# Modulation weights of the feed-forward stage: places of their own, GpSimd's queue, and arithmetic moved to VectorE

## The chip, the cores and the metric

One core of a Trainium2 chip runs the whole program. Its engines are TensorE (PE, with its weight loads as PEld), VectorE (DVE), ScalarE (ACT), GpSimd (POOL) and SyncE (SP). Transfers are issued from the queues of SP, ACT and POOL. The metric is the device time of one execution in microseconds (us); the time of a kernel is the median of its runs.

## What is computed

One step of a two-layer backbone over 384 tokens (128 of context, 256 latent) of width 1024. Each layer is a mixing part and a channel part; the change lies in the channel part and in the modulation that all parts use:

```python
def _modulation(cond, w, b):
    m = jax.nn.silu(cond) @ w + b
    return m.reshape(cond.shape[0], N_MOD, D_MODEL)      # six rows of 1024 for a layer

def _block(x, mod, lw, mix):
    h = _rms(x, g[0]) * (1 + mod[:, None, 1]) + mod[:, None, 0]
    y, aux = mix(h)
    x = x + mod[:, None, 2] * _rms(y @ lw['w_out'], g[1])
    h = _rms(x, g[2]) * (1 + mod[:, None, 4]) + mod[:, None, 3]
    f = jnp.square(jax.nn.relu(h @ lw['ffn_w1'])) @ lw['ffn_w2']
    return x + mod[:, None, 5] * _rms(f, g[3])
```

The weights are float32: w1 and w2 are 1024 x 4096 and 4096 x 1024, and a layer's modulation matrix is 1024 x 6144. Every input is read from HBM once in a run.

## The kernel before, in words

**Dense products.** A float32 weight is cut into units of 128 x 1024 (512 KB). `fetch` (L367) loads a unit into a place named ws or dws (SP, L372), copies it to a rounded high part wh or dwh on ACT, and subtracts to get the low part wl or dwl (`split`, L332 and L320). A product is then three matmuls: high x high, high x low, low x high. The low parts go in turn to the engines in `self.low`: V and P (DVE, POOL) in the dense stages by `P['ld']`, V, V, P in the mixing stage by `P['lm']`. Inside a dense stage the places alternate between a static pool (three ws, two wh, two wl) and one opened by `open_dense` (two dws, four dwh, four dwl).

**The feed-forward stage** (`ffn`, L1670) runs 33 turns. Turn j makes hidden block j with `fm` (24 matmuls of 384 columns into a bank named pd), then Relu on ACT, the square on DVE and a split into f (low part on DVE for even j, on POOL for odd j), and adds hidden block j-1 to the output rows with `rows_product` (18 matmuls of 512 columns into pr and pm). The last four blocks and the norms stand in `dense_end`, which goes through the three tiles of 128 tokens one after another: `postnorm` (residual added half on POOL, half on DVE), then `prenorm` for the next part, whose low parts hl are made on POOL for the first half of the columns.

**Modulation.** One half of a chunk (512 columns of the modulation matrix) is `mod_sums` (L539): four loads of 512 KB into ws and dws places (SP, L545) and eight products with the 32-column cstat; then `mod_turn` copies the sums, transposes them and adds the bias. The first four halves run ahead of layer 0 in `start`, six more halves beside mixing 0. Feed-forward 0 carries twelve halves (chunk 5 of its own layer and five chunks of the next), feed-forward 1 carries two.

**Order.** `merge` interleaves generators by a planner's clock: each yield adds a cost. The modulation generator starts at 28 and its costs are multiplied by 6.5; `presplit` starts at 6 and costs 7.2 a unit. `presplit` loads the 29 input-projection units of layer 1 (SP, L387), splits them and stores the low parts to HBM (SP, L390, the tile low); mixing 1 then loads these. A turn of the feed-forward stage costs 7.8. Each engine and each queue then works through its instructions in a fixed order, and an instruction that waits holds what stands behind it.

In this profile the start lasts to about 33 us, feed-forward 0 runs from 442 to 779 us, and feed-forward 1 from 1156 to 1437 us.

Of the kernel before, what the change touches and what calls it, by code (L numbers as in the profile page):

```python
# [10 lines left out]
F32 = mybir.dt.float32  # L11
# [3 lines left out]
ALU = mybir.AluOpType  # L15
# [153 lines left out]
MIX = (5120, 12544, 15584)  # L169


P = {'wq': [8, 1, 4], 'hp': (0, 400), 'np': 3, 'we': 1, 'dp': [], 'ka': 0, 'kk': [], 'pw': '', 'lm': 'VVP', 'ld': 'VP', 'mf': 6.5, 'pq': [0], 'na': 2, 'nb': 2, 'pe': 'VAVA', 'xw': 4, 'fo': 28, 'wt': 4, 'xs': 2, 'mo': 60, 'mr': 7.5, 'ps': 7.2, 'po': 6, 'rw': (1.4, 1.4), 'ao': (80, 100), 'ar': (1.7, 1.4), 'so': (120, 120), 'sr': (1.4, 1.7), 'ho': (0, 0), 'hr': (0.8, 0.9), 'hl': (4, 4), 'lv': (2.0, 2.0), 'ul': (1, 1), 'rw0': 1.4, 'ao0': 80, 'ar0': 1.7, 'so0': 100, 'sr0': 1.4, 'ho0': 0, 'hr0': 0.9, 'hl0': 6, 'lv0': 4.0, 'ul0': 2, 'rw1': 1.4, 'ao1': 100, 'ar1': 1.7, 'so1': 120, 'sr1': 1.7, 'ho1': 0, 'hr1': 0.9, 'hl1': 4, 'lv1': 2.0, 'ul1': 3}


def par(name, l):
    return P.get(f"{name}{l}", P[name][l])

# [104 lines left out]
class Builder:  # L282
    def __init__(self, nc, tc, pools, io, dbg=None, places=None):
        self.places, self.arenas = places, []
        self.nc, self.tc, self.io, self.dbg = nc, tc, io, dbg
        self.pools = pools
        self.nunit = 0
        self.lows = {}
        self.ready = []
        self.xs, self.xw, self.ntail = P['xw'], 4, 4  # L290
        self.wsets = {n: [(pools[n], n)] for n in ("ws", "wh", "wl")}
        self.turn = {n: 0 for n in self.wsets}
        self.low = (nc.vector, nc.vector, nc.gpsimd)
        self.phase, self.side = None, ExitStack()
# [11 lines left out]
    def pw(self, which):  # L306

        return self.pm() if self.win_left or str(which) not in P["pw"] else self.pd()

# [72 lines left out]
    def presplit(self, l):  # L382

        for n in (7, 8, 0, 2, 4, 1, 3, 5, 6, *range(9, 29)):
            st = self.pools["ws"].tile([128, 1024], F32, name="ws", tag="ws")
            h, lo = (self.pools[k].tile([128, 1024], F32R, name=k, tag=k) for k in ("wh", "wl"))
            self.nc.sync.dma_start(st, self.io["win"][l, n])  # L387
            self.split(h, lo, st)
            d = self.pools["spl"].tile([128, 1024], F32, name=f"low{n}", tag=f"low{n}")
            self.nc.sync.dma_start(d, lo.bitcast(F32))  # L390
            self.lows[l, n] = d
            yield P["ps"]

# [10 lines left out]
    def close(self):  # L404
        if self.phase is not None:
            self.phase.close()
        self.phase = None
        self.static_slots()

    def static_slots(self):  # L410
# [31 lines left out]
    def open_dense(self):  # L442
        self.close()
        self.phase = ExitStack()
        self.low = [{"V": self.nc.vector, "P": self.nc.gpsimd}[x] for x in P["ld"]]
        n = MIX[1] - 4 * 4 * T
        a = self.pool("da", 1)
        self.fy = self.pool("db", 1)
        self.tmp = self.arena([a.tile([128, n], F32, name="tmp")], [n]).get
        p = self.pools  # L450
        for n, k, order in (("ws", self.xs, (0, 1)), ("wh", self.xw, (0, 1, 1)), ("wl", self.xw, (0, 1, 1))):
            q = self.pool("d" + n, k)
            self.wsets[n] = [((p[n], n), (q, "d" + n))[o] for o in order]
# [85 lines left out]
    def mod_sums(self, l, ch, hf):  # L539

        ps = self.pd()
        c0 = ch * 1024 + hf * 512
        for u in range(4):
            w = self.slot("ws", F32)
            self.nc.sync.dma_start(w, self.io["modw"][l, u * 256:u * 256 + 256, c0:c0 + 512].rearrange("(k p) n -> p k n", p=128))  # L545
            for k in range(2):
                n = u * 2 + k
                q = n % 4 * 32
                self.mm(ps[q:q + 32], self.cstat[:, n], w[:, k * 512:k * 512 + 512], n < 4, n >= 4)
        return ps  # L550
# [75 lines left out]
    def norm_out(self, t, q, ps, G, M, h):  # L626
        st = 0 if t == 0 else 1
        hb = self.tmp(512)
        h32 = hb.ap(4, 128)
        for j in range(4):  # L630
            k = q * 4 + j
            c = slice(j * 128, j * 128 + 128)
            if P["pe"][j] == "A":
                self.act(h32[:, j], ps[:, c], AF.Identity, scale=G[:, st, k:k + 1], bias=M[:, st, k:k + 1])
            else:
                self.ts(h32[:, j], ps[:, c], G[:, st, k:k + 1], M[:, st, k:k + 1], ALU.mult, ALU.add)
        sl = (slice(None), slice(q * 4, q * 4 + 4), slice(t * 128, t * 128 + 128))
        self.split(h[0][sl], h[1][sl], h32, self.nc.gpsimd if q in P["pq"] else None)
        hb.free()

    def postnorm(self, t, xt, acc, gate):
        sb = self.tmp(8)
        s = sb.ap(8)
        ub = self.tmp(1024)
        u = ub.ap(1024)
        st = 0 if t == 0 else 1
        for hf in range(2):
            self.act(u[:, hf * 512:hf * 512 + 512], acc[hf], AF.Square, accum_out=s[:, hf:hf + 1])
        self.tt(s[:, 2:3], s[:, 0:1], s[:, 1:2], ALU.add)
        self.rstd(s[:, 3:4], s[:, 2:3], 1.0 / D, 0)  # L650
        for hf in (1, 0):
            sl = slice(hf * 512, hf * 512 + 512)
            self.stt(u[:, sl], acc[hf], s[:, 3:4], gate[:, st, sl])
            self.tt(xt[:, sl], xt[:, sl], u[:, sl], ALU.add, self.nc.gpsimd if hf else None)
        ub.free()
        sb.free()

# [1009 lines left out]
    def wout(self, l):  # L1667
        yield from self.dense_end([self.wout_unit(l, n) for n in (0, 1)], (l, 3), None, [self.io["w1"][l, n] for n in range(P["na"])])

    def ffn(self, l, layers):  # L1670
        nc, io, h = self.nc, self.io, self.h
        fs = [self.fy.tile([128, 4, T], F32R, name=f"f{i}") for i in range(4)]
        self.acc = self.sums("rrrmmm")
        last = l == layers - 1
        tail = []
        for j in range(33):
            if j < 32:
                if j == 0:
                    first = self.fm_first([io["w1"][l, i] for i in range(2)], h)
                o = first[j] if j < 2 else self.fm(io["w1"][l, j], h)  # L1680
                rb = self.tmp(T)
                r = rb.ap(T)
                self.act(r, o, AF.Relu)
                self.tt(r, r, r)
                fh, fl = (fs[j // 4 % 2 * 2 + i][:, j % 4] for i in range(2))
                self.split(fh, fl, r, nc.gpsimd if j % 2 else nc.vector)
                rb.free()
                yield 3.9
            if j:
                n = j - 1  # L1690
                u = (io["w2"][l, n * 128:n * 128 + 128], [fs[n // 4 % 2 * 2 + i][:, n % 4] for i in range(2)])
                if n < 32 - self.ntail:
                    self.rows_product(self.acc, *u[1], self.unit(u[0]), n == 0, False)
                    yield 3.9
                else:
                    tail.append(u)
        self.spread_gate(l, 5)
        save = io["y"] if last else self.pools["dram"].tile([T, D], F32, name="xsave", tag="xsave")
        yield from self.dense_end(tail, None if last else (l + 1, 0), save, [] if last else [self.win_src(l + 1, U_R + n) for n in (7, 8)[:P["nb"]]])
        self.home = save  # L1700

    def build(self, layers=L):
        nc, io = self.nc, self.io
        self.open_x()
        self.open_dense()
        self.home = io["x"]
        self.setup()
        p = self.pools["h"]
        self.h = (p.tile([128, 8, T], F32R, name="hh"), p.tile([128, 8, T], F32R, name="hl"))

        def mod(l, chunks):
            for ch in chunks:
                yield from self.mod_chunk(l, ch)

        def later(chunks):
            for ch in chunks:
                yield from self.mod_chunk(*ch)

        self.start()
        for l in range(layers):  # L1720
            self.mix(l, [(P["mo"], P["mr"], mod(l, (2, 4, 3)), 0)] if l == 0 else [])
            self.run(self.wout(l))
            chunks = [(l, 5)] if l == layers - 1 else [(l, 5)] + [(l + 1, n) for n in (1, 0, 2, 4, 3)]
            self.merge(self.ffn(l, layers), (P["fo"], P["mf"], later(chunks), 0), *([(P["po"], 1.0, self.presplit(l + 1), 0)] if l < layers - 1 else []))
        self.close()
        self.side.close()

# [38 lines left out]
```

## Time and profile before

| | us |
|---|---|
| median of three runs (1448.27 to 1451.86) | 1451.23 |
| the profiled execution's own time | 1446.73 |
| its span, first to last instruction | 1444.9 |
| PE busy | 1297.9 |
| DVE busy | 778.8 |
| ACT busy | 637.6 |
| POOL busy | 396.2 |

The profiled execution is 4.5 us quicker than the median; 1.8 us of its time lie outside the span. Busy time is a sum over the engine's instructions and includes matmuls whose ends are modelled, so a stage is read by what PE waited for and by its pace, not by its busy share alone. A wait is put down to the instruction that came last.

### The profile page before, as it was taken

How to read it: one execution, taken by the hardware profiler on the slowest of the kernel's cores; microseconds unless marked ns; L12 is line 12 of the kernel's file. 1: busy time of each engine (PE TensorE's matmuls, PEld its weight loads, DVE VectorE, ACT ScalarE, POOL GpSimd, SP SyncE). 2: the span in 40 equal slices, each digit the busy share in tenths (PEclk: the TensorE clock that was granted, in tenths of full speed). 3: DMA queues.
4: the chain of work that ended last, by engine and by line, in shares of the span. 5: the costliest groups of instructions: out<-in, count | busy, mean ns of one | idle time of the engine just before them, and what ended most of it. 6: DMA issues, size and time to landing. Idle time of an engine off the chain costs nothing.

```text
span 1444.9 us, 21103 instructions
## 1 busy us (share of the span) xinstructions
PE 1297.9 (90%) x8294; PEld 1090.5 (75%) x8294; DVE 778.8 (54%) x1245; ACT 637.6 (44%) x1255; POOL 396.2 (27%) x288
## 2 busy tenths in 40 slices
PE   6997997899868999999997999879999599999997
PEld 2886686577657777678786988769876498999996
DVE  2689869734443434343544358886454543544443
ACT  4666533244344333344445568333444633333332
POOL 1224536000041123322333003650000422333332
PEclk8998999979986999999998999879999889999999
DMA  9431343621461588888864555216315426544411
GB/s 340 151 105 59 118 126 113 203 91 36 163 205 39 197 297 307 276 313 284 309 236 154 168 186 188 77 29 190 102 39 181 136 67 213 171 129 126 125 59 44
DMA packets 94644, 229.55 MB, mean 159 GB/s; under 512 B 24720, under 2 KB 27088, under 8 KB 94544
## 3 DMA queue, kind: packets, MB, share of 16 engines
q1 hardware_dynamic: 82448, 210.80, 44.0%
q10 hardware_dynamic: 11968, 17.37, 3.7%
q8 instruction: 65, 1.06, 0.3%
q14 instruction: 35, 0.29, 0.1%
q0 software_dynamic: 128, 0.03, 0.0%
HBM read 206.90 MB, written 21.27 MB: 158 GB/s over the span
## 4 chain that ended last, share of the span: by engine, by line
PE 45%; DVE 7%; DMA 7%; ACT 5%; POOL 2%; issue 2%; SPq 0%; ACTq 0%; POOLq 0%; DVEq 0%
PE pd L335 22%; PE pm L335 11%; PE pr L335 11%; DMA ws<-w 3%; DVE mix L320 3%; DMA low<-wl 1%; ACT tmp L329 1%; ACT mix L329 1%; DMA ws<-win 1%; DMA wl<-low 1%; PE pm L338 1%; POOL mix L320 1%; ACT wh L332 1%; ACT dwh L332 1%; DVE wl L320 1%
## 5 line engine op out<-in xcount | busy, mean ns | idle before, releaser
L335 PE MATMUL pd<-hh,wh 128*128 128x384 f32 (+2 forms) x656 | 228.0, 348 | 17.0 <-ACT hh L332 7.2
L335 PE MATMUL pd<-hh,wl 128*128 128x384 f32 (+2 forms) x656 | 227.3, 347 | 13.5 <-DVE wl L320 9.3
L335 PE MATMUL pd<-hl,wh 128*128 128x384 f32 (+2 forms) x656 | 225.5, 344 | 1.3 <-POOL hl L320 1.3
L332 ACT CAST wh<-ws 128x1024 fp32r<-128x1024 f32 x121 | 126.5, 1047 | 174.6 <-DMA ws<-win 70.8
L320 DVE TENSOR_TENSOR tmp<-tmp 128x384 f32<-128x384 f32 (+1 forms) x76 | 101.3, 1333 | 142.5 <-ACT tmp L329 142.4
L320 DVE TENSOR_TENSOR wl<-ws,wh 128x1024 fp32r<-128x1024 f32 x67 | 87.9, 1312 | 132.5 <-ACT wh L332 110.8
L320 DVE TENSOR_TENSOR mix<-mix 128x384 f32<-128x384 f32 (+21 forms) x249 | 143.7, 592 | 28.0 <-ACT mix L329 9.7
L335 PEld LDWEIGHTS pd<-hh,wh 128*128 128x128 f32 x656 | 129.4, 198 | 27.4 <-issue 8.6
L335 PEld LDWEIGHTS pd<-hh,wl 128*128 128x128 f32 x656 | 129.2, 197 | 21.1 <-DVE wl L320 10.3
L329 ACT ACTIVATE mix<-mix 128x384 f32<-128x384 f32 (+4 forms) x188 | 107.4, 599 | 56.6 <-DVE mix L320 34.9
L335 PEld LDWEIGHTS pd<-hl,wh 128*128 128x128 f32 x656 | 129.4, 197 | 3.3 <-POOL hl L320 1.8
L335 PE MATMUL pd<-hh,dwl 128*128 128x384 f32 (+2 forms) x368 | 126.0, 342 | 4.1 <-POOL dwl L320 4.1
L335 PE MATMUL pd<-hh,dwh 128*128 128x384 f32 (+2 forms) x368 | 125.8, 343 | 3.6 <-ACT hh L332 2.7
L335 PE MATMUL pd<-hl,dwh 128*128 128x384 f32 (+2 forms) x368 | 125.4, 341 | 1.8 <-POOL hl L320 1.8
L320 POOL TENSOR_TENSOR wl<-ws,wh 128x1024 fp32r<-128x1024 f32 x25 | 61.6, 2464 | 191.0 <-ACT wh L332 152.7
L320 POOL TENSOR_TENSOR mix<-mix,mix 64x384 f32<-64x384 f32 (+1 forms) x45 | 69.0, 1539 | 88.9 <-ACT mix L329 66.5
L320 POOL TENSOR_TENSOR dwl<-dws,dwh 128x1024 fp32r<-128x1024 f32 x22 | 52.8, 2403 | 125.7 <-ACT dwh L332 125.7
L335 PE MATMUL pr<-dwh,f 128*128 128x512 f32 x252 | 80.4, 400 | 4.1 <-ACT f L332 2.8
L335 PE MATMUL pm<-mix 128*128 128x128 f32 (+5 forms) x700 | 76.0, 268 | 8.5 <-POOL mix L320 5.4
L320 POOL TENSOR_TENSOR dwl<-ws,dwh 128x1024 fp32r<-128x1024 f32 x22 | 53.4, 2427 | 101.2 <-ACT dwh L332 101.2
L332 ACT COPY mix<-pr 32x384 f32<-32x384 f32 (+7 forms) x136 | 42.4, 336 | 83.5 <-PE pr L335 64.8
L335 PE MATMUL pm<-dwh,f 128*128 128x512 f32 x252 | 78.6, 391 | 0.0
(219 smaller groups left out, 2613.7 us busy)
## 6 DMA issues: line engine op xcount, KB each, us to landing
ws<-win SPq DMA_DIRECT2D x87, 512.0 KB, 4.6
dws<-w SPq DMA_DIRECT2D x64, 512.0 KB, 4.5
ws<-w SPq DMA_DIRECT2D x64, 512.0 KB, 4.4
ws<-modw SPq DMA_DIRECT2D x60, 512.0 KB, 4.8
dws<-modw SPq DMA_DIRECT2D x36, 512.0 KB, 6.5
low<-wl SPq DMA_DIRECT2D x29, 512.0 KB, 3.7
wl<-low SPq DMA_DIRECT2D x29, 512.0 KB, 3.7
ws<-wout SPq DMA_DIRECT2D x14, 512.0 KB, 4.1
```

What stands on the lines that cost most here:

```text
L320: (eng or self.nc.vector).tensor_tensor(out, a, b, op=op)
L329: self.nc.scalar.activation(out, a, fn, **kw)
L332: self.nc.scalar.copy(out, a)
L335: self.nc.tensor.matmul(out, l, r, start=start, stop=stop)
L338: self.nc.tensor.transpose(out, a, self.ident[:k, :k])
```

## The change

In the dense stages a pool of four places, wm, holds modulation weights alone, and their loads are issued on GpSimd's queue instead of SP's. That also covers the four halves of `start`, because `build` opens the dense pools before it; the six halves beside mixing 0 still use ws places and SP. In `ffn` the halves are no longer a merged generator: from turn 3 on every odd turn takes one half, its sums ahead of `rows_product` and its turning behind it, so that feed-forward 0 does its twelve in turns 3 to 25 and feed-forward 1 its two in turns 3 and 5. The store of presplit's low parts moves from SP's to GpSimd's queue. The low parts of dense units (`P['ld']` goes from 'VP' to 'V'), of f and of hl, and the residual add, all go to VectorE. The keys mf, fo and pq leave the table P. GpSimd's arithmetic in the mixing stage stays.

```diff
@@ presplit
-            self.nc.sync.dma_start(d, lo.bitcast(F32))
+            self.nc.gpsimd.dma_start(d, lo.bitcast(F32))
@@ close
-        self.phase = None
+        self.phase = self.wmod = None
@@ open_dense
+        self.wmod = self.pool("wm", 4)
         p = self.pools
@@ mod_sums
-            w = self.slot("ws", F32)
-            self.nc.sync.dma_start(w, self.io["modw"][l, u * 256:u * 256 + 256, c0:c0 + 512].rearrange("(k p) n -> p k n", p=128))
+            if self.wmod is not None:
+                w = self.wmod.tile([128, 1024], F32, name="wm", tag="wm")
+                q = self.nc.gpsimd
+            else:
+                w, q = self.slot("ws", F32), self.nc.sync
+            q.dma_start(w, self.io["modw"][l, u * 256:u * 256 + 256, c0:c0 + 512].rearrange("(k p) n -> p k n", p=128))
@@ norm_out
-        self.split(h[0][sl], h[1][sl], h32, self.nc.gpsimd if q in P["pq"] else None)
+        self.split(h[0][sl], h[1][sl], h32)
@@ postnorm
-            self.tt(xt[:, sl], xt[:, sl], u[:, sl], ALU.add, self.nc.gpsimd if hf else None)
+            self.tt(xt[:, sl], xt[:, sl], u[:, sl], ALU.add)
@@ ffn
-                self.split(fh, fl, r, nc.gpsimd if j % 2 else nc.vector)
+                self.split(fh, fl, r)
                 rb.free()
+                mod = halves.pop(0) if halves and j > 2 and j % 2 else None
+                if mod:
+                    ps = self.mod_sums(*mod)
                 yield 3.9
...
                     self.rows_product(self.acc, *u[1], self.unit(u[0]), n == 0, False)
+                    if mod:
+                        self.mod_turn(*mod, ps)
                     yield 3.9
@@ build
-            chunks = [(l, 5)] if l == layers - 1 else [(l, 5)] + [(l + 1, n) for n in (1, 0, 2, 4, 3)]
-            self.merge(self.ffn(l, layers), (P["fo"], P["mf"], later(chunks), 0), *([(P["po"], 1.0, self.presplit(l + 1), 0)] if l < layers - 1 else []))
+            chunks = [(l, 5)] + [(l + 1, n) for n in (1, 0, 2, 4, 3)] * (l < layers - 1)
+            self.merge(self.ffn(l, layers, [(*c, hf) for c in chunks for hf in range(2)]),
+                       *([(P["po"], 1.0, self.presplit(l + 1), 0)] if l < layers - 1 else []))
```

## Rows read from the trace of the kernel before

**Rows 1.** The page: PE's busy tenths in 40 slices of 36.1 us

```profile
PE   6997997899868999999997999879999599999997
```

**Rows 2.** Stretches: length, busy PE, PEld, DVE, ACT, POOL, clock, DMA share, GB/s

```profile
12.00:24.00 12.00, 9.24 (x60) 3.99 (x58) 4.29 (x23) 6.86 (x17) 0.00 (x0) 1.00 1.05 401
...
460.00:770.00 310.00, 297.37 (x1511) 240.45 (x1511) 130.28 (x133) 122.06 (x162) 89.18 (x47) 0.99 0.79 271
490.00:740.00 250.00, 237.74 (x1213) 187.39 (x1206) 108.87 (x112) 103.27 (x135) 74.05 (x39) 1.00 0.86 299
...
1162.00:1424.00 262.00, 262.00 (x1366) 235.83 (x1365) 120.11 (x86) 90.08 (x128) 86.68 (x47) 1.00 0.38 123
```

**Rows 3.** PE's waits from 454 to 770 us: total, times, longest

```profile
PE pd L335 <- POOL dwl L320: 4.1, 3, 1.5
PE pr L335 <- ACT f L332: 2.8, 2, 1.8
```

**Rows 4.** Waits of SP's DMA queue, 454 to 790 us

```profile
SPq L390 <- DVE wl L320: 80.4, 23, 10.1
...
SPq L545 <- POOL dwl L320: 18.2, 5, 5.7
```

**Rows 5.** Modulation matmuls (tile cstat): both feed-forward stages; PE busy is first

```profile
454.00:790.00 336.00, 29.52 (x192) 5.62 (x192) 0.00 (x0) 0.00 (x0) 0.97 0.75 258
1160.00:1300.00 140.00, 3.85 (x32) 0.83 (x32) 0.00 (x0) 0.00 (x0) 0.99 0.46 149
```

**Rows 6.** The chain in feed-forward 1, two pieces sixteen turns apart

```profile
1256.76 4.17 PE pd L335 x24
...
1390.52 4.24 PE pd L335 x24
```

**Rows 7.** Groups from 454 to 790 us: busy, mean ns, idle before

```profile
L320 POOL TENSOR_TENSOR dwl<-ws,dwh 128x1024 fp32r<-128x1024 f32 x20 | 48.6, 2429 | 98.4 <-ACT dwh L332 98.4
...
L320 DVE TENSOR_TENSOR dwl<-dws,dwh 128x1024 fp32r<-128x1024 f32 x19 | 35.9, 1908 | 31.4 <-ACT dwh L332 31.4
...
L320 POOL TENSOR_TENSOR wl<-ws,wh 128x1024 fp32r<-128x1024 f32 x9 | 22.5, 2496 | 57.8 <-ACT wh L332 50.4 <-DMA ws<-win 7.5
...
L320 POOL TENSOR_TENSOR f<-tmp,f 128x384 fp32r<-128x384 f32 x16 | 17.2, 1073 | 66.9 <-ACT f L332 66.9
```

**Rows 8.** Timeline: one low part on DVE while POOL is idle

```profile
487.67 1.23 DVE L320 TENSOR_TENSOR wl<-ws,wh 128x1024 fp32r<-128x1024 f32 x1 [3.95 <-ACT wh L332]
```

**Rows 9.** PE's waits, 400 to 460 us: total, times, longest

```profile
PE pd L338 <- DVE tmp L326: 14.6, 1, 14.6
...
PE pd L335 <- POOL hl L320: 1.8, 2, 0.9
```

**Rows 10.** Timeline inside the wait of 14.6 us

```profile
429.25 2.34 POOL L320 TENSOR_TENSOR wl<-ws,wh 128x1024 fp32r<-128x1024 f32 x1
429.77 4.65 DVE L320 TENSOR_TENSOR x<-x,tmp 128x512 f32<-128x512 f32 x3
```

**Rows 11.** PE's waits, 1105 to 1165 us

```profile
PE pd L335 <- POOL wl L320: 3.5, 2, 2.7
```

**Rows 12.** Timeline ahead of that wait

```profile
1120.17 4.83 POOL L320 TENSOR_TENSOR dwl<-dws,dwh 128x1024 fp32r<-128x1024 f32 x2 [8.10 <-ACT dwh L332]
...
1124.96 2.35 POOL L320 TENSOR_TENSOR wl<-ws,wh 128x1024 fp32r<-128x1024 f32 x1
```

**Rows 13.** The start: landing of its 16 modulation loads (tile modw, 0 to 36 us)

```profile
DMA to landing us min/median/max: 4.6/7.9/10.8
```

**Rows 14.** Timeline of the start: last sums, first dense product

```profile
30.39 1.06 PE L335 MATMUL pd<-ws,cstat 128*32 128x512 f32 x2
...
32.72 0.69 PE L335 MATMUL pd<-hh,wh 128*128 128x384 f32 x1 [0.40 <-ACT wh L332]
```

**Rows 15.** Landing of modulation loads, 454 to 790 us (tile modw)

```profile
DMA to landing us min/median/max: 3.9/5.6/8.8
```

**Rows 16.** GpSimd's only transfers before, 8 KB each: ns min, median, max

```profile
L593 POOL DMA_DIRECT2D gates<-grow x4: 522/546/677, 199.1 to 1239.1; - x4
```

More of the change, by code (lines that the diff above doesn't have):

```diff
@@ L169 @@
 MIX = (5120, 12544, 15584)
-P = {'wq': [8, 1, 4], 'hp': (0, 400), 'np': 3, 'we': 1, 'dp': [], 'ka': 0, 'kk': [], 'pw': '', 'lm': 'VVP', 'ld': 'VP', 'mf': 6.5, 'pq': [0], 'na': 2, 'nb': 2, 'pe': 'VAVA', 'xw': 4, 'fo': 28, 'wt': 4, 'xs': 2, 'mo': 60, 'mr': 7.5, 'ps': 7.2, 'po': 6, 'rw': (1.4, 1.4), 'ao': (80, 100), 'ar': (1.7, 1.4), 'so': (120, 120), 'sr': (1.4, 1.7), 'ho': (0, 0), 'hr': (0.8, 0.9), 'hl': (4, 4), 'lv': (2.0, 2.0), 'ul': (1, 1), 'rw0': 1.4, 'ao0': 80, 'ar0': 1.7, 'so0': 100, 'sr0': 1.4, 'ho0': 0, 'hr0': 0.9, 'hl0': 6, 'lv0': 4.0, 'ul0': 2, 'rw1': 1.4, 'ao1': 100, 'ar1': 1.7, 'so1': 120, 'sr1': 1.7, 'ho1': 0, 'hr1': 0.9, 'hl1': 4, 'lv1': 2.0, 'ul1': 3}
+P = {'wq': [8, 1, 4], 'hp': (0, 400), 'np': 3, 'we': 1, 'dp': [], 'ka': 0, 'kk': [], 'pw': '', 'lm': 'VVP', 'ld': 'V', 'na': 2, 'nb': 2, 'pe': 'VAVA', 'xw': 4, 'wt': 4, 'xs': 2, 'mo': 60, 'mr': 7.5, 'ps': 7.2, 'po': 6, 'rw': (1.4, 1.4), 'ao': (80, 100), 'ar': (1.7, 1.4), 'so': (120, 120), 'sr': (1.4, 1.7), 'ho': (0, 0), 'hr': (0.8, 0.9), 'hl': (4, 4), 'lv': (2.0, 2.0), 'ul': (1, 1), 'rw0': 1.4, 'ao0': 80, 'ar0': 1.7, 'so0': 100, 'sr0': 1.4, 'ho0': 0, 'hr0': 0.9, 'hl0': 6, 'lv0': 4.0, 'ul0': 2, 'rw1': 1.4, 'ao1': 100, 'ar1': 1.7, 'so1': 120, 'sr1': 1.7, 'ho1': 0, 'hr1': 0.9, 'hl1': 4, 'lv1': 2.0, 'ul1': 3}
 def par(name, l):
@@ L287, in __init__ @@
         self.nunit = 0
-        self.lows = {}
+        self.lows, self.wmod = {}, None
         self.ready = []
@@ L1668, in wout, with ffn @@
         yield from self.dense_end([self.wout_unit(l, n) for n in (0, 1)], (l, 3), None, [self.io["w1"][l, n] for n in range(P["na"])])
-    def ffn(self, l, layers):
+    def ffn(self, l, layers, halves):
         nc, io, h = self.nc, self.io, self.h
@@ L1696, in ffn @@
                     tail.append(u)
+        assert not halves
         self.spread_gate(l, 5)
@@ L1713, in mod @@
                 yield from self.mod_chunk(l, ch)
-        def later(chunks):
-            for ch in chunks:
-                yield from self.mod_chunk(*ch)
         self.start()
```

## The prediction

> **What bounds the kernel now.** I read the page's slices first: PE is at nine tenths or more wherever a feed-forward stage runs, and low in the first slice, near slice 12 and at the changes of stage [rows 1]. The stretches by window then separate two cases. Feed-forward 1 between 1162 and 1424 us has PE busy for all of its 262 us, with the DMA engines at 0.38 [rows 2]: nothing off PE can shorten it. Its pace is steady: sixteen turns between two pieces of the chain, (1390.52 - 1256.76)/16 = 8.36 us a turn [rows 6]. Feed-forward 0 does the same products, yet between 460 and 770 us PE is idle for 310 - 297.4 = 12.6 us, with the DMA engines at 0.79, and at 0.86 from 490 to 740 us [rows 2]. Its clock is 0.99 to 1.00 of full there, so no term below is a clock term. The list of waits says for what PE stood: low parts on POOL first, then f and low parts on DVE [rows 3]. The waits of SP's queue show why operands come late: the store of presplit's low part stood at the head of that queue for 80.4 us in 23 waits, and modulation loads for another 18.2 us behind POOL's low parts [rows 4]. Everything behind them, dense weights above all, was issued late. So the change can act on feed-forward 0, on the joints between stages, and on the start.
>
> **Dense turns of feed-forward 0.** SP loses the 48 modulation loads and 29 stores; its ws places serve dense and presplit units alone. A low part leaves POOL, where it took 2.43 to 2.50 us, for DVE, where it takes 1.23 us [rows 7, 8]. DVE gains 20 + 9 units x 1.23 = 35.7 us and f's sixteen low parts, at most the 17.2 us that POOL needed [rows 7, 8]. It was busy for 130.3 us of 310, so it gets to at most 183, some 60%. It also gets time back: its own dwl took 1.91 us on average against 1.23 us with POOL idle [rows 7, 8], on nineteen units about 13 us. DVE thus covers what it is given; a cover that failed would show as PE waiting for DVE low parts. Of the 12.6 us of idle PE the change can win all or nothing; I take 7, because waits for ACT and for landings remain [rows 3].
>
> **Modulation matmuls.** Sums whose weights lie ready cost 3.85/2 = 1.92 us a half (feed-forward 1); feed-forward 0 spent 29.5 us on twelve halves, against 12 x 1.92 = 23.1 us [rows 5]. The difference, 6.4 us, is weights that came one after another, so that only some of the column groups ran together. After the change the next half's four loads go out as the previous half's matmuls free the places, and have two turns, 16.7 us [rows 6], against a landing of at most 8.8 us in this stage [rows 15]. I take 6 (between 0 and 6.4).
>
> **The joints.** At the end of the output projection of layer 0 PE waits for 14.6 us on the norms, then 1.8 us for hl on POOL [rows 9]. Inside, a presplit low part on POOL and three residual adds on DVE run against each other: the adds take 1.55 us each [rows 10], where half a unit's columns would be some 0.6 us at the rate of the clean row (half of 1.23) [rows 8]. Without POOL's work I estimate 3 us here; the adds that POOL did are then in line on DVE, so it may also be 0. In layer 1 PE waits 2.7 us for a low part that stood behind two dense ones on POOL, 4.83 us together [rows 11, 12]; these two leave POOL, so most of that goes. With hl's, I take 5 in all (0 to 8). The last norms before y have the same adds, without a cover; there one more add stands in line on DVE, and the output waits for it: I take 0.
>
> **The start.** Its sixteen modulation loads have four places instead of five and POOL's queue instead of SP's. SP is then free at once for three input-projection units. These come earlier than needed and share the DMA engines, which are full (401 GB/s between 12 and 24 us) [rows 2]: 1.57 MB are 3.9 us later for the last modulation load. The last sums ran at 30.4 us, the first dense product began at 32.7 us [rows 14]; the second waits for such a unit, the first sets the second half of h. I take +3. It may be -2, if the early units are what counts, or much more if POOL issues slowly. No row shows a 512 KB load there: the nearest are the four gate stores, 0.52 to 0.68 us each [rows 16]; I take 0.55, since sixteen such issues fit easily into 30 us; a much higher price is the third rival's.
>
> **Costed at nothing.** Feed-forward 1: PE is saturated, and DVE's added splits run beside it. The places of wm take room from the mixing tiles: their first loads wait for mixing to end, three turns before they are used. The order of POOL's queue: below.
>
> **The sum** is -7 - 6 - 5 + 3 = -15 us, from 1446.7 us of the profiled execution to 1432. That execution is 4.5 us under the median of 1451.2 us, so by the median I predict 1436.
>
> **The rivals.**
> First, the DMA engines are the limit of feed-forward 0. From 490 to 740 us they moved 299 GB/s x 250 us = 74.8 MB at a share of 0.86; without 12.3 us of idle PE and some 5 us of late modulation that is 321 GB/s, a share of 0.92 [rows 2]. For it: bursts of four modulation loads now compete with dense loads instead of standing behind them. Against it: the start held 401 GB/s. If dense weights come as late as before, the first two terms are 0: -2 at the joints and +3 at the start give 1452, no change.
> The Trainium skill, page "Trainium Kernel Development and Optimization", section "Key Constraints", speaks for this one: transfers issued from SP, ACT and POOL run on the same 16 engines, and issuing from several only saves the sequencer's issue time. By it alone the queue is worth nothing and the time is this rival's; the stretch rows agree that the engines are nearly full, but SP's waits for a store, which are no transfer time, are not in that rule.
>
> Second, the side of loss: POOL's queue takes over the wait. A modulation load now waits for the previous half's matmuls, up to two turns, and the stores of presplit and the gates stand behind it. A held store holds a wl place; the static pool has two, and every third dense unit needs one, so PE waits for that unit's low part. Every half can do this once, twelve times; the gains of 18 us in feed-forward 0 and the joints, less 3, are gone when each is 15/12 = 1.3 us of idle PE, and half a turn each, 12 x 4.2 = 50 us, gives 1436 + 50 = 1486. A mild case, 2.5 us each, gives 1466. For it: the store already was the longest wait of SP's queue [rows 4]. Against: on SP it stood behind more loads than that.
>
> Third, POOL's loads are slow at the start. Four places need four rounds; a round is landing, 1.05 us of sums and 0.55 us of issue. At 10.8 us, the longest landing of the start [rows 13], that is 49.6 us against the 30.4 us of before: 19 us instead of 3, and 1452. Above 12 us a landing it is slower than before.
> The Trainium skill, "SBUF — State Buffer", section "SBUF: two separate sides", has a way for that: descriptors of a transfer from GpSimd are written by GpSimd itself, and VectorE's two-port modes lock it out meanwhile. No row here shows it.
>
> Fourth, the same reasons in full: no idle PE in feed-forward 0, all joints clean, start neutral: -12.6 - 6.4 - 8 = -27, 1424.
>
> That wm is not used is excluded by the text: `build` and `mix` open the dense pools ahead of every such sum.
>
> **How the numbers follow.** The forecast has 0.46 (its own range 1428 to 1444), the first rival 0.19, the second 0.15, the third 0.08, the fourth 0.12. A difference of 0.3%, 4.4 us, is about what a measurement of this kernel can tell from none. Faster: the forecast, the fourth and 0.07 of the first (a gain that is partly kept), 0.65. Same: 0.12 of the first and 0.03 of the third, 0.15. Slower: the second and 0.05 of the third, 0.20. The range leaves out the lower half of the fourth and the worse part of the second: 1422 to 1460.
>
> **What would show it.** Right: PE's idle time between turns 1 and 29 of feed-forward 0 falls to about 5 us; cstat there is near 23 us; SP's wait for a store is gone; dwl on DVE is 1.2 us; PE's longest wait after the output projection of layer 0 is about 11 us; the first dense product begins between 30 and 37 us. Wrong: POOL's queue holding a store for matmuls while PE waits for wl; a DMA share above 0.95 with PE waiting for casts; modulation landings above 12 us at the start.

## The result, and the profile after

The changed kernel takes 1433.05 us (median of 5 runs, 1427.74 to 1436.41) where the kernel before took 1448.27 us in the runs beside it (5 runs, 1442.61 to 1451.86): a ratio of 0.9886, 95% interval 0.9855 to 0.9916. The forecast was 1436 us. The profiled execution after spans 1431.2 us against 1444.9, so 13.7 us are to be found; -15 was the sum. Some executions of any of these kernels run at a lower granted clock and take over 1.5% longer than the kernel's fastest; the ratios here and below leave them out, the medians do not.

PE's busy tenths on the page of the kernel after, to be read beside [rows 1]:

```profile
PE   5897998899985999999997999869999699999997
```

The first slice fell from 6 to 5: the start is longer. The joint before feed-forward 0, which reads 8, 6, 8 from slice 11 in [rows 1], reads 9, 8, 5: it comes later, and PE is at work in every slice of the turns behind it, as before.

The stretches after, with the columns of [rows 2]; the second and the first answer to its rows of feed-forward 0, the last to feed-forward 1:

```profile
480.00:730.00 250.00, 248.90 (x1325) 204.71 (x1324) 125.01 (x162) 110.08 (x144) 47.45 (x73) 1.00 0.88 316
470.00:765.00 295.00, 293.82 (x1553) 245.16 (x1553) 142.56 (x189) 126.81 (x177) 47.45 (x73) 1.00 0.78 278
1150.00:1412.00 262.00, 261.91 (x1364) 235.57 (x1363) 107.32 (x134) 93.85 (x131) 3.40 (x5) 1.00 0.36 115
```

PE's idle time in the turns of feed-forward 0 is down from 12.6 us to 1.2 (295.00 - 293.82), while the DMA engines carry 316 GB/s at a share of 0.88: they are no limit. DVE holds 48% of its time, where the prediction allowed 60%. Feed-forward 1 is saturated as before.

The modulation matmuls after (tile cstat; PE's busy time first, as in [rows 5]), and the low parts on DVE, as in [rows 7]:

```profile
440.00:790.00 350.00, 25.37 (x192) 5.14 (x192) 0.00 (x0) 0.00 (x0) 0.95 0.70 249
1150.00:1290.00 140.00, 3.85 (x32) 0.83 (x32) 0.00 (x0) 0.00 (x0) 1.00 0.43 139
```

```profile
L320 DVE TENSOR_TENSOR dwl<-ws,dwh 128x1024 fp32r<-128x1024 f32 x20 | 24.5, 1224 | 34.2 <-ACT dwh L332 34.2
L320 DVE TENSOR_TENSOR dwl<-dws,dwh 128x1024 fp32r<-128x1024 f32 x20 | 24.2, 1219 | 8.5 <-ACT dwh L332 8.5
```

The twelve halves fell from 29.5 to 25.4 us, not to 23.1. The low part costs DVE 1.22 us now, as expected.

PE's waits after, first from 380 to 460 us (they answer to [rows 9]), then from the first product of feed-forward 0 to the end of its turns, 457 to 765 us ([rows 3]), then at the joint of layer 1, 1090 to 1155 us ([rows 11]):

```profile
PE pd L338 <- DVE tmp L326: 6.6, 1, 6.6
PE pm L338 <- DVE tmp L326: 6.2, 1, 6.2
...
PE pd L335 <- ACT hh L332: 3.1, 1, 3.1
PE pd L335 <- ACT tmp L329: 1.1, 1, 1.1
...
PE pd L335 <- POOL wl L320: 1.1, 2, 0.8
```

Where one wait of 14.6 us for the norms stood there are now two, 6.6 and 6.2; those for hl on POOL are gone. The 3.1 us for hh still belong to the joint (2.7 before), so the turns are left with a single wait of 1.1 us.

The start after: the landing of its sixteen loads ([rows 13]), and the timeline at the first dense product ([rows 14]):

```profile
DMA to landing us min/median/max: 4.1/6.1/15.1
```

```profile
38.68 0.44 PE L335 MATMUL pd<-hh,wh 128*128 128x384 f32 x1
...
42.72 1.05 PE L335 MATMUL pd<-wm,cstat 128*32 128x512 f32 x4 [0.56 <-DMA wm<-modw]
```

The first dense product came 6.0 us later than before (38.7 against 32.7), and the last sums of the start now run behind it (42.7 us against 30.4).

From the timelines of both kernels, stage by stage (us; a stage ends with the matmul that is named):

| stage | before | after | difference |
|---|---|---|---|
| start, to the first dense product | 32.7 | 38.7 | +6.0 |
| mixing 0, to the end of its output projection | 388.8 | 398.6 | +9.8 |
| joint, to the first product of f | 48.4 | 40.0 | -8.4 |
| turns of feed-forward 0, to the last product of f | 309.0 | 288.4 | -20.6 |
| end of feed-forward 0 | 13.1 | 12.9 | -0.2 |
| mixing 1, to the end of its output projection | 346.8 | 348.5 | +1.7 |
| joint | 38.3 | 36.9 | -1.4 |
| feed-forward 1 and y | 267.8 | 267.2 | -0.6 |

The pieces add up to the 13.7 us. The gain in the turns is larger than forecast, and a loss of 9.8 us in mixing 0 was in no term.

### The profile page after: what moved, and what is told of

It reads as the page before. It is cut to its first block, busy times and chain, and to the rows that moved or that the text cites. A ratio compares the mean times of both kernels' runs of the same rounds, so it can differ in the third digit from the quotient of the medians.

```text
span 1431.2 us, 21075 instructions
## 1 busy us (share of the span) xinstructions
PE 1295.2 (90%) x8294; PEld 1088.7 (76%) x8294; DVE 779.8 (54%) x1367; ACT 639.9 (45%) x1255; POOL 240.1 (17%) x267
## 4 chain that ended last, share of the span: by engine, by line
PE 69%; DVE 14%; DMA 6%; ACT 5%; issue 3%; POOL 1%; SPq 0%; ACTq 0%; DVEq 0%; POOLq 0%
PE pd L335 33%; PE pr L335 17%; PE pm L335 16%; DVE mix L320 7%; DMA wm<-modw 2%; PE pm L338 2%; ACT mix L329 2%; ACT tmp L329 2%; DVE wl L320 1%; DMA mix<-inv 1%; DVE mix L323 1%; ACT wh L332 1%; DMA inv<-mix 1%; PE pr L338 1%; DMA ws<-win 1%
## 5 line engine op out<-in xcount | busy, mean ns | idle before, releaser
L320 DVE TENSOR_TENSOR mix<-mix 128x384 f32<-128x384 f32 (+21 forms) x249 | 139.8, 577 | 32.7 <-ACT mix L329 11.6
L320 DVE TENSOR_TENSOR wl<-ws,wh 128x1024 fp32r<-128x1024 f32 x78 | 98.1, 1258 | 102.8 <-ACT wh L332 64.6
L335 PEld LDWEIGHTS pd<-hh,wl 128*128 128x128 f32 x656 | 127.9, 195 | 20.7 <-DVE wl L320 12.7
L335 PE MATMUL pd<-hh,dwl 128*128 128x384 f32 (+2 forms) x368 | 122.9, 334 | 0.0
L320 DVE TENSOR_TENSOR dwl<-ws,dwh 128x1024 fp32r<-128x1024 f32 x44 | 53.9, 1225 | 70.4 <-ACT dwh L332 70.3
L320 DVE TENSOR_TENSOR dwl<-dws,dwh 128x1024 fp32r<-128x1024 f32 x44 | 53.5, 1221 | 58.8 <-ACT dwh L332 58.8
L550 POOL DMA_DIRECT2D wm<-modw x72 | 52.0, 725 | 196.9 <-PE pd L335 146.2
L335 PE MATMUL pr<-dwh,f 128*128 128x512 f32 x252 | 80.4, 397 | 0.0
L335 PE MATMUL pm<-mix,mix 128*128 128x64 f32 (+4 forms) x468 | 75.6, 302 | 1.7 <-ACT mix L332 1.6
```

What stands on the lines that cost most here:

```text
L320: (eng or self.nc.vector).tensor_tensor(out, a, b, op=op)
L335: self.nc.tensor.matmul(out, l, r, start=start, stop=stop)
L550: q.dma_start(w, self.io["modw"][l, u * 256:u * 256 + 256, c0:c0 + 512].rearrange("(k p) n -> p k n", p=128))
```

## The experiments

Within one kernel the time goes with the mean granted clock of an execution (the kernel before: 1439.8 us at 0.947, 1458.8 us at 0.928). Over 117 executions of all these kernels a line through each kernel's own scatter falls by 1.0 us for each 0.001 of clock. The table gives the median, the ratio to the runs of the kernel before beside it (their medians are 1448.27 to 1449.95 us), and the mean that this line gives at a clock of 0.941, an estimate of mine: a change may move the clock itself, and then the column takes away a part of its effect. Then come the first dense product, the turns of feed-forward 0, PE's idle time in them and the busy time of tile cstat there, all of one profiled execution. Two more profiles of the changed kernel gave turns of 289.7 and 291.6 us, one more of the kernel before 311.1, so a difference of 3 us in that column says nothing.

| kernel | median us | ratio, 95% interval | at 0.941 | first product | turns | PE idle | cstat |
|---|---|---|---|---|---|---|---|
| before | 1448.27 | 1 | 1448.0 | 32.7 | 309.0 | 12.6 | 29.5 |
| after | 1433.05 | 0.9886 (0.9855 to 0.9916) | 1434.1 | 38.7 | 288.4 | 1.2 | 25.4 |
| e1 old start | 1419.61 | 0.9795 (0.9762 to 0.9828) | 1423.3 | 32.4 | 288.6 | 1.3 | 25.4 |
| e2 transfers on SP | 1429.26 | 0.9837 (0.9792 to 0.9882) | 1426.7 | 34.5 | 284.2 | 0.0 | 23.1 |
| e3 GpSimd arithmetic back | 1455.75 | 1.0008 (0.9973 to 1.0044) | 1452.9 | 36.2 | 299.8 | 8.1 | 24.1 |
| e4 arithmetic alone | 1427.23 | 0.9827 (0.9792 to 0.9861) | 1432.1 | 32.4 | 293.1 | 0.9 | 28.5 |
| e5 e1 and e2 together | 1413.93 | 0.9755 (0.9706 to 0.9803) | 1419.1 | 32.5 | 284.2 | 0.0 | 23.1 |
| e6 no places, SP | 1446.97 | 0.9987 (0.9960 to 1.0015) | 1445.4 | 32.6 | 306.0 | 11.2 | 28.5 |
| e7 e5, GpSimd kept busy | 1419.62 | 0.9804 (0.9758 to 0.9850) | 1426.4 | 32.6 | 284.5 | 0.2 | 23.1 |
| e9 e5, GpSimd arithmetic back | 1429.68 | 0.9855 (0.9800 to 0.9909) | 1426.2 | 32.5 | 284.7 | 0.0 | 23.3 |
| e10 e5, dense low parts back | 1425.55 | 0.9833 (0.9783 to 0.9882) | 1424.9 | 32.5 | 286.8 | 1.2 | 23.3 |

**e1: the start as before.** The wm pool is opened from feed-forward 0 on, so the start's halves use ws and dws places and SP.

```diff
@@ __init__
-        self.lows, self.wmod = {}, None
+        self.lows, self.wmod, self.fed = {}, None, False
@@ open_dense
-        self.wmod = self.pool("wm", 4)
+        self.wmod = self.pool("wm", 4) if self.fed else None
@@ build
         self.start()
+        self.fed = True
```

> The changed kernel with one part undone: the four halves of the start use ws and dws places and SP's queue again, as before the change; wm opens with the first feed-forward stage. In the changed kernel the first dense product begins at 38.7 us against 32.7 before, and mixing 0 then ends 15.8 us later than before, so some 10 us more are lost inside mixing 0. Theory A (the start's queue and places cost 6 us, and the other 10 are mixing 0's order and clock that follow from the late start): the first product is back near 33 us, the joint behind mixing 0 near 422 us, and the time is 10 to 16 us below the changed kernel, 1418 to 1423, ratio to before 0.979 to 0.982. Theory B (the 10 us in mixing 0 have nothing to do with the start): first product near 33 us, but only 6 us below the changed kernel, 1427, ratio 0.984. Theory C (the start costs nothing in the end, since mixing waits for something else): 1433.

The first dense product is back at 32.4 us, the turns stay at 288.6, and the ratio is 0.9795, its interval clear of the changed kernel's. The time is that of this run's theory A: the new start is a loss. Its mechanism is not: mixing 0 stayed at 398.7 us, so its length does not come from the late start, as theory B has it. Of the 11 us between the two at one clock, the first product shows 6.3; where the rest lies stays open.

**e2: both transfers back on SP,** the places kept.

```diff
@@ mod_sums
-                q = self.nc.gpsimd
+                q = self.nc.sync
@@ presplit
-            self.nc.gpsimd.dma_start(d, lo.bitcast(F32))
+            self.nc.sync.dma_start(d, lo.bitcast(F32))
```

> The changed kernel with both transfers back on SP's queue (modulation loads and presplit's stores); wm keeps its four places, the turns and the arithmetic stay as changed. Theory A (own places and fixed turns are the gain, the queue is worth little): feed-forward 0 keeps its gain of some 20 us, with PE idle under 5 us between 480 and 730 us, and the time is within 4 us of 1433. Theory B (SP's head-of-line waits were the cause, so the queue is the gain): SP waits some 80 us for low parts again, PE idle in feed-forward 0 is back at 10 us or more, the time is 1440 to 1448. The start may gain up to 6 us in either, as its loads are issued by SP in order ahead of the projection units.

SP's queue from 440 to 780 us, and the stretch of the turns:

```profile
SPq L390 <- DVE wl L320: 76.2, 21, 9.3
```

```profile
468.00:752.00 284.00, 284.00 (x1511) 238.61 (x1510) 139.11 (x183) 122.73 (x171) 1.03 (x2) 1.00 0.79 287
```

The store's wait at the head of SP's queue is back almost whole (80.4 us in [rows 4]), and PE has no idle time at all, as theory A has it. The longest of the waits on which the prediction built its cause is harmless here. The turns even gain 4.2 us on the changed kernel: cstat falls by 2.3 us to 23.1, the floor that [rows 5] gave, and the idle 1.2 us go. The loads of the stage land in 6.6 us in the middle here and in 7.9 us from GpSimd's queue:

```profile
DMA to landing us min/median/max: 3.9/6.6/11.5
```

```profile
DMA to landing us min/median/max: 4.1/7.9/13.5
```

These are tile modw, 440 to 790 us, in e2 and in the changed kernel.

**e3: GpSimd's arithmetic back,** in the changed kernel.

```diff
-'ld': 'V'
+'ld': 'VP'
-                self.split(fh, fl, r)
+                self.split(fh, fl, r, nc.gpsimd if j % 2 else nc.vector)
@@ norm_out
-        self.split(h[0][sl], h[1][sl], h32)
+        self.split(h[0][sl], h[1][sl], h32, self.nc.gpsimd if q == 0 else None)
@@ postnorm
-            self.tt(xt[:, sl], xt[:, sl], u[:, sl], ALU.add)
+            self.tt(xt[:, sl], xt[:, sl], u[:, sl], ALU.add, self.nc.gpsimd if hf else None)
```

> The changed kernel with GpSimd's arithmetic of the dense stages back (dense low parts in turn on DVE and POOL, f of odd turns, hl of the first half, half of the residual adds). POOL's loads and stores then stand behind its arithmetic. Theory A (the move to VectorE is worth the joints and part of the idle PE, as predicted: some 5 us at the joints and 3 to 5 in the turns): 1440 to 1444, with PE waiting for POOL low parts again. Theory B (own places carry all): within 4 us of 1433. Theory C (arithmetic on POOL delays the modulation loads now issued there): over 1446.

The whole gain is gone: 1.0008, as theory C has it. Waits of POOL, 455 to 765 us:

```profile
POOL dwl L320 <- ACT dwh L332: 58.5, 13, 9.7
POOL low L390 <- DVE wl L320: 42.4, 11, 7.9
POOL f L320 <- ACT f L332: 21.7, 9, 6.4
POOL low L390 <- DVE mod L320: 16.0, 5, 5.8
```

Here low parts and transfers hold each other up in one queue: a store that waits for DVE holds the dwl behind it, and a dwl that waits for its cast holds the next loads. PE is idle for 8.1 us of 299.8.

**e4: the arithmetic alone,** in the kernel before: the four edits of e3 the other way round, nothing else.

> The kernel before with the arithmetic alone moved to VectorE; modulation stays a merged generator on ws places and SP's queue. Theory A: joints shorter by some 5 us and fewer waits for POOL in feed-forward 0, 1440 to 1444, ratio 0.993 to 0.997; modulation matmuls stay near 29.5 us, SP's 80 us wait for the store stays. Theory B (arithmetic carries most of the gain): 1435 or less. Theory C (nothing without the places): 1446 to 1450.

Theory B, that the arithmetic carries the gain, holds. Without places and without GpSimd's queue the ratio is 0.9827; at one clock, 1432.1 us, it equals the changed kernel. The turns, where PE's idle time falls from 12.6 to 0.9 us with the transfers on SP as before:

```profile
467.00:760.00 293.00, 292.07 (x1511) 238.32 (x1510) 139.35 (x182) 124.48 (x171) 1.03 (x2) 1.00 0.80 285
```

SP's queue there, 454 to 790 us, to be read beside [rows 4]:

```profile
SPq L390 <- DVE wl L320: 64.2, 22, 9.2
...
SPq L545 <- PE pd L335: 23.6, 10, 8.1
SPq L545 <- DVE dwl L320: 12.4, 11, 2.4
```

So the store and the modulation loads still stand at the head of that queue, and PE waits for hardly anything behind them.

cstat stays at 28.5 us. That makes 28.5 - 23.1 = 5.4 of the 8.9 us by which these turns are longer than the best of 284.2.

**e5: e1 and e2 together:** DVE arithmetic, places in the feed-forward stages alone, both transfers on SP.

> The changed kernel with its start as before (ws and dws places, SP) and both transfers on SP's queue; what is left of the change is the arithmetic on VectorE, the four places of feed-forward modulation and the fixed turns. Theory A (POOL's queue costs 4 us in the turns and the start's four places cost 6 us, and the two add up): feed-forward 0's turns take 284 us as with the queue alone undone, first dense product near 32.5 us, 1412 to 1418 in all, ratio 0.974 to 0.979, the best so far. Theory B (the start's loss is taken back by what follows, so only one of the two counts): 1420 to 1426.

The best of all, 1413.93 us and 0.9755, ahead of both kernels, as theory A has it: the two gains add. Its turns are those of e2, its start that of before.

**e6: no places.** The changed kernel with `self.wmod = None` throughout and the store on SP: the fixed turns and DVE's arithmetic remain, the halves load into the dense places.

> The run before this one without places of its own: the halves keep their fixed turns and the arithmetic stays on VectorE, but modulation weights go through ws and dws places on SP again (the store of the low parts too). Theory A (own places make the four weights of a half lie ready; their matmuls take 23.1 us with places on SP's queue and 28.5 us without, as the arithmetic alone has them): modulation matmuls 28 us or more, feed-forward 0's turns near 293 us, 1420 to 1427. Theory B (the fixed turns do it, places are not needed): matmuls near 23 us, turns near 284 us, 1412 to 1418.

Nothing is left of the gain: 0.9987. The modulation matmuls take 28.5 us, as theory A has it, but the turns are longer than either theory said. PE's waits in the turns, 472 to 780 us:

```profile
PE pd L335 <- ACT dwh L332: 7.1, 5, 2.7
PE pr L335 <- ACT wh L332: 1.2, 1, 1.2
```

Both are high parts of dense weights that came late. Four modulation loads taken at a fixed point of a turn occupy dense places; with the generator of before, which spread them (e4), PE's idle time was 0.9 us, here 11.2. So halves at fixed turns need places of their own; fast low parts are not enough for them. Places of their own under the old generator were not run, so "places" below means places with fixed turns.

**e7: e5 with GpSimd kept busy.** For every second dense unit GpSimd makes a useless subtraction of 128 x 1024 whose result nobody reads; everything else is computed as in e5.

```diff
@@ fetch
+        if self.idle is not None and self.nunit % 2:
+            self.tt(self.idle, h.bitcast(F32), self.cst[:, 0:1024], ALU.subtract, self.nc.gpsimd)
```

> The kernel of e5 with useless work added on GpSimd: for every second dense unit of the feed-forward stages (and of presplit none) a subtraction of 128 x 1024 with two SBUF inputs, of the unit's high part and a constant, into a scratch tile that nobody reads. VectorE still makes every low part. It tells why GpSimd's arithmetic cost time before. Theory A (contention: a two-input operation on GpSimd holds up VectorE's two-input operations): VectorE's low parts go from 1.22 to 1.8 us or more on average, and if that was the cost, some of the 12 us of idle PE returns and the time rises by 4 us or more. Theory B (latency: a low part on GpSimd came 2.4 us after the high part instead of 1.2, and VectorE's slowing was harmless): VectorE's low parts are slower, but PE stays at work and the time is within 3 us of e5.

DVE's low parts from 440 to 790 us (1223 and 1220 ns in e5), with GpSimd's own:

```profile
L321 POOL TENSOR_TENSOR idle<-dwh,cst 128x1024 f32<-128x1024 f32 x20 | 62.0, 3100 | 132.2 <-ACT dwh L333 132.1
...
L321 DVE TENSOR_TENSOR dwl<-dws,dwh 128x1024 fp32r<-128x1024 f32 x19 | 33.8, 1797 | 5.3 <-ACT dwh L333 5.3
L321 DVE TENSOR_TENSOR dwl<-ws,dwh 128x1024 fp32r<-128x1024 f32 x20 | 33.3, 1665 | 14.6 <-ACT dwh L333 14.6
```

On average DVE's low parts are 36 to 47% slower. The single ones (shortest, median and longest in ns) show that most are not slowed at all and some take nearly three times as long:

```profile
L321 DVE TENSOR_TENSOR dwl<-ws,dwh x20: 1212/1226/3431, 457.3 to 722.0; 128x1024 fp32r<-128x1024 f32 x20
L321 DVE TENSOR_TENSOR dwl<-dws,dwh x19: 1208/1214/3432, 455.7 to 711.4; 128x1024 fp32r<-128x1024 f32 x19
```

The turns stay at 284.5 us, as theory B has it: with places of their own there is room for DVE's slower pace. But with them the turns also bear low parts on POOL (e9, below), so this run does not tell which of the two, contention or the longer low part, cost time in the kernel before. The time is 5.7 us above e5 by the medians (7.3 at one clock), which is theory A's, and not in the turns; in the profiles the two joints are longer, 40.5 against 37.1 us and 39.1 against 36.3. What lengthens them was not tested.

**e8: the changed kernel again.**

> The changed kernel once more, unaltered, for a second profile of the same program beside the others. Mixing 0 and the start ended 15.8 us later than before in the first profile, 6 of them at the start. Theory A (the late end is the program's own, from its order of work): again 435 to 439 us at the end of the output projection of layer 0, ratio 0.985 to 0.992. Theory B (the clock in mixing 0 differs from execution to execution): the end moves by 5 us or more, the granted clock between 39 and 437 us with it.

1431.19 us, ratio 0.9862 (0.9809 to 0.9916). The first product came at 38.2 us and the turns took 289.7: both reproduce. The end of the output projection does not: it came at 450.8 us, mixing 0 took 412.6 us instead of 398.6, and this profiled execution took 1446.13 us at a mean clock of 0.932 (0.78 between 345 and 400 us, where the first profile has 1.00). That is theory B's, not A's.

**e9: e5 with all of GpSimd's arithmetic back.** The diff of e3 on top of e5.

> The best version so far (own places in feed-forward 0, both transfers on SP, start as before) with all of the arithmetic given back to GpSimd: low parts of every second dense unit, of odd f, of the first half of hl, and the residual add. Theory A (what counts is the latency of operands on GpSimd, 2.4 us a low part against 1.2; the places are worth only what the modulation matmuls gain): the arithmetic's return costs some 10 us in the turns and joints, so the turns of feed-forward 0 take about 295 us, cstat stays near 23 to 24 us, PE waits again for POOL low parts, and the time is about 1432 us, ratio near 0.988. Theory B (places on SP's queue take the modulation loads out of the dense places, which alone makes operands early enough for either engine): turns 284 to 287 us, and a ratio near 0.980. Theory C (the places have no worth of their own without the arithmetic, on whichever queue): ratio near 1.000, turns above 300 us.

The turns, 478 to 763 us:

```profile
478.00:763.00 285.00, 284.83 (x1510) 238.21 (x1508) 129.42 (x140) 122.54 (x170) 89.26 (x48) 1.00 0.80 285
```

In the turns theory B holds: 284.7 us, with the dense low parts back on POOL at 2.44 us, f's at 1.11 us, and no wait of PE. The places, on SP's queue and with fixed turns, are enough by themselves. The time is not B's, though: 7 us more than e5 at one clock. The joint before the turns shows a large part of that. The first three columns are the stretch, its length and PE's busy time; PE's granted clock is the third from the end. e9:

```profile
463.00:475.00 12.00, 12.00 (x59) 12.00 (x59) 3.87 (x4) 3.27 (x5) 2.23 (x1) 0.57 0.14 45
```

and the same place of e10, where hl is on DVE:

```profile
460.50:472.50 12.00, 11.93 (x77) 11.15 (x77) 6.40 (x7) 4.84 (x8) 2.52 (x1) 1.00 0.29 87
```

In both PE is busy all the time, but in e9 it runs mostly at 1.2 GHz (0.57), and gets through 59 matmuls instead of 77. Ahead of it, in e9, stands a wait for hl on POOL:

```profile
462.75 0.33 PE L335 MATMUL pd<-hl,dwh 128*128 128x128 f32 x1 [0.91 <-POOL hl L320]
```

From the first product of feed-forward 0 to the first product of f, e9 takes 26.6 us, e10 20.3 and e5 21.0. The kernel before has the same pair, a wait of 0.91 us for hl and then 0.57 over 12 us (27.4 us; 26.7 in its second profile), and so has e3 (23.5 us). Of the ten profiles with hl on DVE only e6 has the second fall (26.0 us), and there PE waited 0.3 us for hl, as in e4 and e10, which do not have it. So the fall can come without hl on POOL.

**e10: e5 with the dense low parts alone back** (`'ld': 'VP'`).

> The best version so far with only every second dense unit's low part given back to GpSimd; the low parts of f and of hl and the residual add stay on VectorE. Theory A (the low parts of weights are the arithmetic that counts in the turns): turns as in the run with all of the arithmetic back, about 295 us; only the joint before feed-forward 0 is shorter than there, by 2 to 4 us; ratio near 0.986. Theory B (f's low part counts, since it stands between fm and rows_product with one turn of slack, while weights come early): turns 284 to 287 us, ratio 0.976 to 0.979.

1424.9 us at one clock, so between e5 (1419.1) and e9 (1426.2); the intervals of e9 and e10 overlap, and their order is not settled. Turns 286.8 us, which is theory B's; the joint is short. The ratio, 0.9833, is above B's. The dense low parts cost the turns 2.6 us at most once the places are there.

**e11 and e12: the kernel before and the changed kernel again,** for mixing 0.

> The kernel before, unaltered, for a second profile. Open is the 9.8 us that mixing 0 (first dense product to the last matmul of the output projection) was longer after the change, 398.6 against 388.8 us, with a granted clock of 0.89 against 0.92 between 40 and 340 us. Theory A (the clock of mixing 0 differs from one execution to the next, whatever the kernel): mixing 0 of this profile lies anywhere from 388 to 400 us, and its length goes with the granted clock of 40 to 340 us. Theory B (the change makes mixing 0 longer): it is within 2 us of 388.8, at a clock near 0.92. The start (first dense product at 32.7) and the turns of feed-forward 0 (309 us) should come back within 1 us and 3 us under either.

> The changed kernel, unaltered, for a third profile, beside the second one of the kernel before. Theory A (the clock of mixing 0 differs from one execution to the next): mixing 0 between 388 and 400 us, longer where the granted clock of 40 to 340 us is lower. Theory B (the change makes it longer): 397 to 400 us again, at a clock of 0.88 to 0.90. The start should come back near 38.5 us and the turns near 289 us.

These are single executions, 1446.17 and 1436.03 us. The turns came back at 311.1 and 291.6 us (309.0 and 288.4 in the first profiles), the first products at 32.6 and 39.0. Mixing 0 took 386.6 us in e11 and 398.1 us in e12, against 388.8 and 398.6: in these four each kernel repeats itself, as theory B has it. But e8 took 412.6 us with the same program as e12, and e9, whose TensorE instructions stand in the same order as those of before up to the output projection, took 398.9 us. The stretch from 290 to 330 us, before and e9:

```profile
290.00:330.00 40.00, 37.03 (x433) 29.82 (x432) 14.30 (x41) 18.56 (x54) 1.03 (x2) 0.79 0.25 83
```

```profile
290.00:330.00 40.00, 37.84 (x326) 29.62 (x326) 10.80 (x29) 16.41 (x46) 1.06 (x2) 0.57 0.27 86
```

PE is busy as long in both, at a granted clock of 0.79 and of 0.57, and gets through 433 and 326 matmuls. In the changed kernel the clock is 0.65 there. So most of the 10 us is time at the lower clock near the end of mixing 0, and e9 shows that it can come without a change of what TensorE does there. What makes that stretch longer stays open. Two things speak against the parts of the change as the cause: e9 has the arithmetic and the start of before, and e7, with all of DVE's arithmetic, took 388.4 us. That the change made mixing 0 longer is not shown.

## Why the prediction was right, and where not

The total was right, 1436 for 1433 us, and the sum's own -15 stands against -13.7, but that is partly luck: the turns and joints gave 12 us more than was forecast, and the start and mixing 0 took 13 us more.

**Dense turns and modulation matmuls** (-7 and -6): -20.6 together, with PE idle for 1.2 us instead of the 5 that was expected (12.6 before), and cstat 4.1 us shorter instead of 6 (the other 2.3 come with SP's queue, e2). These are 15.5 us; the other 5 stand in PE's busy time, whose ends are modelled, and I do not attribute them. The size was missed because more waits ended than the forecast let end.

**The cause was the step that failed:** "The waits of SP's queue show why operands come late ... Everything behind them, dense weights above all, was issued late." The larger half of that, the store, is refuted. In e2, e5 and e9 it stands at the head of SP's queue for 76.2, 75.6 and 63.4 us and PE waits for nothing; in e4, with shared places, for 64.2 us, and PE is idle for 0.9. The smaller half, modulation loads that hold that queue, is at most a part of the cause: in e4 they still wait there for matmuls and low parts, and PE does not. With the arithmetic on DVE and halves at fixed turns in the dense places PE is idle for 11.2 us all the same (e6). So the idle time of before came from GpSimd's arithmetic and modulation loads in the dense places together. There are two cures, each sufficient:

| turns, us | shared places, SP | own places, GpSimd's queue | own places, SP |
|---|---|---|---|
| arithmetic partly on GpSimd | 309.0 (before) | 299.8 (e3) | 284.7 (e9) |
| arithmetic all on DVE | 293.1 (e4) | 288.4 (after) | 284.2 (e5) |

The first column has the generator of before, the others have fixed turns. The arithmetic on DVE ends the waits without any new place (e4); whether by low parts of 1.2 us instead of 2.4, or because GpSimd no longer slows DVE, was not separated. Places of their own end the waits with GpSimd's low parts of 2.4 us (e9); the dense places are then left to dense units. In the turns both together gain hardly more than the places alone. The third part of the change, GpSimd's queue, is a loss in either row: 288.4 - 284.2 = 4.2 us with DVE's arithmetic, 299.8 - 284.7 = 15.1 us without.

**The first rival** is refuted: 316 GB/s at a share of 0.88 with PE at work. Its own sum took 2 us for the joints where the forecast took 5; with 5 it gives 1449, which is still no change. The rule of the Trainium skill beside it ("Trainium Kernel Development and Optimization", "Key Constraints"), that issuing from several queues only saves issue time, agrees in so far as the queue gave nothing. Here it cost more: a load's issue took 0.72 us on GpSimd and 0.37 us on SP in the start, and what stands in that queue now waits with it (e3).

**The second rival,** GpSimd's queue as the new wait, exists without the loss that was priced. The store waits there after the change, in the list of POOL's waits from 440 to 780 us:

```profile
POOL low L390 <- DVE wl L320: 148.3, 18, 40.0
POOL wm L550 <- PE pd L335: 64.9, 13, 8.8
```

The store waits 40 us once, mostly at the joint, and PE does not notice: no operand of a dense unit stands behind it in that queue. With arithmetic in the same queue PE is idle for 8.1 us (e3): the rival lacked that condition.

**The start** (+3, and the third rival's +19): +6.0. An issue took 0.72 us, not 0.55, the first product at 38.7 us lay outside the 30 to 37 that were named, and the longest landing, 15.1 us, was above the 12 us named as a bad sign; but the median of 6.1 us was below the 7.9 of before. The last sums came 12.3 us later than before, the first product only 6.0, since it no longer stands behind them. The first sums ran at 10.8 us, on SP in e2 at 5.7: three input-projection units, issued from SP at once, share the DMA engines with the first loads of GpSimd. By the first product, places cost 2.0 us (e2 against e5) and the queue 4.2 (after against e2).

**The joints** (-5): -8.4 and -1.4. The two waits for the norms sum to 12.8 us after 14.6 (12.7 in the second profile of before), so of the 3 us priced for the adds at most 1.8 show; 2.7 us for wl became 0.8, near the step. The large part had no term: before, PE ran at 1.2 GHz a second time, for some 10 us behind the wait for hl, and in the changed kernel it does not. With the waits for hl, priced at 1.8 us, that makes 7.2 us of the joint (27.4 against 20.2 from the first product to the first of f; 6.3 in e9 against e10). The prediction read the clock in the turns alone, where it is 0.99 to 1.00, and concluded that "no term below is a clock term". That hl's wait brought the fall on is not shown (e6).

**Mixing 0** was in no term: +9.8 us at a lower clock, come back in e12, more in e8 (412.6 us), and open in its cause. Without it the change would have been near the fourth case.

## What to carry to other kernels

A queue's long wait names the instruction that stands there, not what PE lacks: put the transfer elsewhere and look whether PE's waits go before building on it. Where one engine's queue carries both arithmetic and transfers, each of its waits holds both; move one of them, and prefer the queue that does no arithmetic. Of a change in several parts run each part alone: here the arithmetic alone carried the whole gain, the places with fixed turns would have carried as much, and GpSimd's queue was a loss hidden beneath them.

## What was not expected of the hardware

A wait of 0.91 us of TensorE for the low parts of h was followed by a second stretch at 1.2 GHz, some 10 us long, in all four profiles that have it; a wait of 0.3 us or none at the same place was not, in nine of ten. The tenth, e6, had the fall with the same 0.3 us as e4 and e10. That is a coincidence shown often, not a mechanism shown.

With GpSimd at work on two inputs beside it, DVE's dense low parts of 1.22 us took 1.67 and 1.80 us on average (e7), but not evenly: of the 39 most stay at 1.21 to 1.23 us and nine take 3.42 to 3.43. GpSimd took 3.10 us for its subtraction there, 2.40 at the least, where low parts of the same size took it 2.44 us in e9. The Trainium skill ("SBUF — State Buffer", "SBUF: two separate sides") says that a DVE instruction with two inputs in SBUF and a GpSimd instruction that reads SBUF take turns at a shared pair of ports; the rows agree in that some of DVE's operations last about as long as both together and the others lose nothing. In the turns of e7 it cost PE nothing.
